# A hybrid decoder layer on one core: reordering the last K step of the input projection, and starting two branches inside it

## Chip, core and metric

The kernel runs on one core of a Trainium2 chip. The metric is the device time of one execution in microseconds (us); lower is better. Three runs of the kernel before gave 1704.4, 1707.65 and 1708.73 us, so the median is 1707.65 us.

## What is computed

One decoder layer on 256 prompt tokens and 8 sample tokens (264 columns), model width 2048, everything in float32. Cut to what matters here:

```python
mod = silu(c) @ w_mod + b_mod                      # six sections of 2048
h = rmsnorm(x, g_mix) * (1 + sc_m) + sh_m
proj = h @ w_in                                    # u_a, u_b, v_b, z, xbc, dt, three gates
o_a = s5_branch(u_a, ...)                          # scan over time, then y * sigmoid(y @ w_glu)
o_b = gelu(u_b) * (w_s @ rmsnorm(gelu(v_b)) + b_s) # gMLP
o_c = ssd_branch(z, xbc, dt, ...)                  # conv, chunked scan, gate, norm
merged = g_a*(o_a @ w_pa) + g_b*(o_b @ w_pb) + g_c*(o_c @ w_pc)
x = x + gt_m * (merged @ w_out)
x = x + gt_f * conv_ffn(rmsnorm(x) * (1 + sc_f) + sh_f)
```

## The kernel before

**Weights.** Activations lie with features on partitions and the 264 tokens along the free dimension. A weight piece is 512 KB (four k tiles of 128 by 256 columns). `load_w` (line 284) loads it through SP into one of three `raw` buffers; ACT copies it to `hi` (line 255 is the helper `act`) and DVE, or POOL for every second piece of the streams named in `SHARED` (`w_pb`, `w_ga`, `w_pa`, `w_z`), subtracts to get `lo` (line 243, helper `sub`). `gemm_piece` (305) then issues 24 matmuls of 264 columns: hi by xh, hi by xl, lo by xh (line 258, helper `mm`). `prefetch` keeps loads and splits three pieces ahead.

**K steps.** The first part of the input projection cannot wait for the whole normalised input, because the modulation that it needs is itself computed from streamed weights. So it runs in the five steps of `KSTEPS` (line 36): k tiles 0-1, 2-3, 4-7, 8-11, 12-15. Each step goes through all 16 column groups of 256 and a narrow one, `DT` (64), in the order given by `cuts` (67), and adds its part to the accumulators `acc` (0 to 2 hold xbc, 3 u_a, 4 v_b, 5 u_b, 6 and 7 the first half of the gate of branch B) on DVE (line 240, helper `add`). In a step, the modulation of the next four k tiles is loaded and multiplied (`mod_gen`, 369).

**The rest.** After the last K step come the streams `w_gb` (16 pieces here), `w_pb` (8), `w_ga` (32), `w_pa` (8), `w_z` (16), `w_gc`, `w_pc`, `w_out`, then the feed-forward part. The other four sections of the modulation run beside them (`mod_sec`, 387; its matmuls are named `mods`).

**Background work.** The branches are Python generators in the queue `fill`, run strictly one after the other. `pump` (449) is called behind each piece with a credit in us; it issues generator steps, each with its own price (`yield 2.3`), until the credit is used; `yield BRK` ends the turn. `finish` (463) issues all that is left of one. A K step of four k tiles gives 0.3 x 4 = 1.2 us per group (1198), the streams behind it 2.2 us per piece (`PACE`, 1246). The generators touched here:

- `gen_s5_prep` (556): constants of S5, small DVE operations, loads of 128, 512 and 512 KB through SP, eight PE transposes. Queued in the step with k0 = 8 (1176).
- `gen_s5_tables` (640): four tables of cosines and sines, built by 168 POOL operations. Queued in the last step (1178), completed behind it (1206).
- `gen_gm` (775): the gMLP branch. Two loads (512 and 256 KB), a POOL select, gelu on ACT, the norm, four transposes `vT` and 16 matmuls `gms` per half.
- `gen_s5` (666): 16 state tiles. Per tile PE reads in (4 matmuls `pg<-acc,bbT`), DVE rotates (`ta<-pg`, `tb<-pg`), scans (line 733) and rotates back together with POOL (`s5hh`), PE reads out (`s5py`). A tile is priced 1.3 + 2.3 + 0.6 us and has a `BRK`. Behind the last tile: gelu, the split into `s5h` and `s5l`, and two pieces of `w_glu`, loaded when they are reached (765), not ahead.
- `gen_ssd` (830): convolution of xbc, the softplus and cumulative sum of dt, then two chunks.

`gen_gm`, `gen_s5` and `gen_ssd` are queued in this order behind the last K step (1242 to 1244); `finish(g_gm)` stands ahead of `w_pb`, `finish(g_s5)` ahead of `w_pa`, `finish(g_ssd)` behind `w_z`. All engine orders come out of a scheduler at build time that works through this program order by priority, with buffers and estimated durations; each engine then runs its list in order.

Of the kernel before, what the change touches and what calls it, by code (L numbers as in the profile page):

```python
# [36 lines left out]

# ---------------------------------------------------------------- host layout

# [12 lines left out]
def _feat(a):  # L52
    """(F,) -> [128, F/128], feature on partitions."""
    return np.asarray(a).reshape(-1, P).T


def _pieces(w, kk):
    """[K, N] -> [N/256 * K/(128 kk), 128, kk*256], column groups outermost."""
    K, N = w.shape
    a = w.reshape(K // (P * kk), kk, P, N // 256, 256).transpose(3, 0, 2, 1, 4)  # L60
    return np.ascontiguousarray(a).reshape(-1, P, kk * 256)
# [4 lines left out]

def cuts(nk):
    """Column groups of one step (DT: the narrow one), in pieces of at most four k tiles x groups."""
    n = 4 // nk
    out = [[DT]]  # L70
    for lo, hi in ((0, 6), (6, 12 + NGA)):
        out += [list(range(a, min(a + n, hi))) for a in range(lo, hi, n)]
    return out[1:] + out[:1]


def pack(i):
# [22 lines left out]
    for s, (k0, nk) in enumerate(KSTEPS):  # L99
        r = slice(P * k0, P * (k0 + nk))  # L100
        v = [np.concatenate([dtp[r] if g == DT else wa[r, 256 * g:256 * g + 256] for g in gs], 1)
             for gs in cuts(nk)]
        A[f"w_a{s}"] = np.concatenate([a.reshape(nk, P, -1).transpose(1, 0, 2).reshape(-1) for a in v])
# [89 lines left out]

# ---------------------------------------------------------------- the kernel

def build(tc, I, O):
# [57 lines left out]
    def act(o, a, f, **kw):  # L254
        S.activation(o, a, f, **kw)  # L255
# [3 lines left out]

    # ---- constants  # L260
    ident = cst.tile([P, P], F32, name="ident")
# [20 lines left out]

    # ---- helpers
    def load_w(src, kk, n, e=V):
# [15 lines left out]
    def take():  # L300
        """Next piece of the main stream; loads and splits run ahead of its use."""
        prefetch()
        return ahead.popleft()

    def gemm_piece(ps, w, X, k0, kk, nt, start, stop, c0=0):
        """ps[:, j, :T] += W[k0.., tile j]^T X, W and X each in two f32r parts."""
        hi, lo = w
        for j in range(nt):
            c = slice(c0 + 128 * j, c0 + 128 * j + 128)
            for i in range(kk):  # L310
                xh, xl = X(k0 + i)
                o = ps[:, j, :T]
                mm(o, hi[:, i, c], xh, start and i == 0, False)
                mm(o, hi[:, i, c], xl, False, False)
                mm(o, lo[:, i, c], xh, False, stop and i == kk - 1)

    def rstd_of(ps, n, width=T):
        """1/sqrt(ps/n + eps), one Newton step after the table."""
        v = W("rv", [P, width])
        ts(v, ps, 1.0 / n, ALU.mult, EPS, ALU.add)  # L320
        y = W("ry", [P, width])
        act(y, v, AF.Sqrt)
        V.reciprocal(y, y)
        t = W("rt", [P, width])
        stt(t, y, -0.5, y, ALU.mult, ALU.mult)
        mult(t, t, v)
        r = W("rstd", [P, width])
        stt(r, t, 1.5, y, ALU.add, ALU.mult)
        return r
# [4 lines left out]

    # ---- modulation
    mod_ps, mod_ev = {}, {}

    def mod_load(s_, nk, sec, i):
        """8 / nk k tiles of 128 nk columns"""
        raw = RM("rawm")  # L340
        nc.sync.dma_start(raw, I[f"w_m{s_}"][2 * nk * sec + i])
        return raw.rearrange("p (k n) -> p k n", k=8 // nk)
# [26 lines left out]
    def mod_gen(s_, k0, nk, depth):  # L369
        """sc, then sh, of nk feature tiles, at least four k tiles per step; the loads run ahead of their use."""  # L370
        pp = max(2, nk // 2)
        steps = [(sec, i) for sec in (1, 0) for i in range(0, 2 * nk, pp)]
        got = deque()
        for j in range(len(steps) + depth):
            if j < len(steps):
                sec, i = steps[j]
                got.append([mod_load(s_, nk, sec, i + p_) for p_ in range(pp)])
            if j >= depth:
                sec, i = steps[j - depth]
                for p_, raw in enumerate(got.popleft()):  # L380
                    mod_part(sec, i + p_, nk, raw)
                if i + pp == 2 * nk:
                    with tc.high_priority():
                        mod_fin(sec, k0, 128 * nk)
            yield pp / max(1, nk // 2)

    def mod_sec(sec, depth=1, get=RM, kk=2):
        """One section of 2048 columns, kk k tiles per step; its four 512-column chunks sit in four column groups."""
        ps = None
# [33 lines left out]
    def modulate(k0, nk, xq, rstd, gname, s_sh, s_sc, hi, lo):  # L423
        """hi + lo = x * rstd * (g (1 + sc)) + sh for feature tiles k0.. k0+nk-1 (of one slot)"""
        sh = mod[:, 16 * s_sh + k0:16 * s_sh + k0 + nk, :]
# [18 lines left out]

    # ---- background work, paced against the weight pieces
    fill = deque()
# [42 lines left out]

    # ---- first RMS norm  # L490
    rstd0 = cst.tile([P, T], F32, name="rstd0")

    def sum_tok(pt, sqs, first, last):
        """sums of squares, tokens on partitions; the three columns share a bank, so only the first starts"""
        for i, sq in enumerate(sqs):
            for b, t0 in enumerate((0, 128, T - 128)):
                mm(pt[:, b:b + 1], sq[:, t0:t0 + 128], ones[:, :1], first and i == 0 and b == 0,
                   last and i == len(sqs) - 1)
        return pt

    def rstd_tok(pt, PM=PM):
        """1/sqrt(mean + eps) of every token, on all partitions, by way of tokens on partitions"""
        w = W("rtk", [P, 4, 3])
# [25 lines left out]

    # ---- S5: parameters  # L530
    def exp_acc(o, a, n):
# [130 lines left out]

    # ---- branch A: S5
    oA = {}
# [108 lines left out]

    # ---- branch B: gMLP
    def gen_gm(ub, vb):
# [50 lines left out]

    # ---- branch C: SSD
    xsb = {}

    def gen_ssd(raws, dtr):  # L830
# [29 lines left out]

        # dt = softplus(raw + bias), da = -exp(a_log) dt
        dt = cst.tile([16, T], F32, name="dt")
# [47 lines left out]
        yield BRK  # L910
        # token-major B, CB^T
        Bt = W("Bt", [P, 2, 2, 128])
# [175 lines left out]

    # ---- segment A: modulated norm and the first column tiles, one quarter of K at a time
    XH, XL, acc = [], [], []  # L1090
# [3 lines left out]
    for s_, (k0, nk) in enumerate(KSTEPS):  # L1094
        o = 0
        for i, gs in enumerate(cuts(nk)):
            n = 128 if gs == [DT] else 256 * len(gs)
            e = G if (i % 2 == 1 if nk == 1 else i % 3 == 1 and nk == 2) else V
            queue.append((I[f"w_a{s_}"][o:o + P * nk * n].rearrange("(p n) -> p n", p=P), nk, n, e))
            o += P * nk * n  # L1100
# [3 lines left out]
    def lead_order(n):  # L1104
        """the first groups side by side, one piece of K after the other"""
        m = KD // 4
        return [g * m + q for q in range(m) for g in range(LEAD)] + list(range(LEAD * m, n))
# [30 lines left out]
    def warm(n, src=None):  # L1138
        """matmuls that keep the tensor engine's clock up while the first loads arrive"""
        for _ in range(n):  # L1140
# [27 lines left out]
    for s_, (k0, nk) in enumerate(KSTEPS):  # L1168
        nxt = None
        if s_ + 1 < NS:  # L1170
            nxt = step_mods(s_ + 1)
            mods.append(nxt)
            if s_ == 0:
                prefetch()
                mpump(DEPTH(1))
        if k0 == 8:
            fill.append(g_prep)
        if s_ == NS - 1:
            fill.append(g_tab)
        for g, first, o in [(g, i == 0, 256 * i) for gs in cuts(nk) for i, g in enumerate(gs)]:  # L1180
            ps = PG()
# [14 lines left out]
            if s_ == NS - 1 and g >= 12:  # L1196
                act(dst, dst, AF.Sigmoid)
            pump(0.3 * nk)
            mpump(0.8 if KSTEPS[min(s_ + 1, NS - 1)][1] > 1 else 0.8 / 2)
# [3 lines left out]
        if nxt:  # L1203
            mfinish(nxt)
            step_h(s_ + 1)
    finish(g_tab)

    # ---- the rest of the input projection, with the branches behind it
    MS = (1, RM, 2) if 2 == 2 else (2, RM, 1)
# [31 lines left out]

    g_s5, g_gm = gen_s5(acc[3]), gen_gm(acc[5], acc[4])
    g_ssd = gen_ssd(acc[:3], acc_dt)
    fill.extend([g_gm, g_s5, g_ssd])

# [48 lines left out]

    # ---- output projection, residual
    x1 = [Q("x1") for _ in range(4)]
    for j in range(4):
        nc.sync.dma_start(x1[j], I["x"][j])
    def residual(g, src, xt, s_gt, ssq, scale=None):
        """xt += gate * src for two feature tiles; sums of squares, then the scaling of the final norm"""  # L1300
        c0 = 2 * (g % 2)
# [49 lines left out]

    # ---- ConvFFN
    AH, AL = {}, {}
# [78 lines left out]
```

## Time and profile before

| | |
|---|---|
| median of three runs | 1707.65 us (1704.4 to 1708.73) |
| span of the profiled execution, first to last instruction | 1703.2 us |
| its own time with what lies around the span | not given apart from the runs, whose lowest is 1704.4 us |
| busy PE, DVE, ACT, POOL | 1655.1, 1125.4, 735.0, 285.6 us |
| weight loads on PE (PEld) | 1523.5 us |
| last K step, `w_gb`, S5 tiles, `w_pa` in this trace | about 230 to 279, 279 to 341, 315 to 468, 523 to 557 us |

The span is read as one line of time from 0 to 1703.2 us. An engine's busy time says how long it had an instruction in work; a matmul's row runs from its start to its modelled end, and matmuls overlap, so the distance of starts is the pace. "idle before <-" tells what ended an engine's idle time.

### The profile page before, as it was taken

What the parts mean: (1) busy time and instruction counts of PE and PEld (TensorE: products, weight loads), DVE (VectorE), ACT (ScalarE), POOL (GpSimd) and SP (SyncE); (2) the same over time, 40 slices, a digit from 0 to 9 for tenths busy, and PEclk for the clock granted to TensorE, in tenths of its full rate; (3) what the DMA queues carried; (4) which work ended last, traced back from release to release, by engine and by line L of the source; (5) the groups of instructions that cost most, each with busy time, mean ns of one, the idle gap of its engine ahead of it and who ended that gap; (6) DMA issues with size and microseconds to landing.
All of it is one profiled execution on the core that took longest, in us unless ns stands there. A gap on an engine that the chain in (4) does not pass through costs nothing.

```text
span 1703.2 us, 32237 instructions
## 1 busy us (share of the span) xinstructions
PE 1655.1 (97%) x13172; PEld 1523.5 (89%) x13172; DVE 1125.4 (66%) x1897; ACT 735.0 (43%) x962; POOL 285.6 (17%) x323
## 2 busy tenths in 40 slices
PE   7999999999999999999999999999999999999996
PEld 5778899877777799999988999999999999999996
DVE  3455877899969648875547766666544566666553
ACT  4423346322255533354335544545433455455442
POOL 0200079266734324200000000000000000000000
PEclk8999999999999999999999999999999999999998
DMA  8867985666467857868995666545555555555552
GB/s 319 303 230 289 342 286 168 223 244 226 165 215 269 303 210 259 287 213 299 332 348 195 241 217 225 177 174 194 178 185 180 179 186 181 182 185 182 181 185 89
DMA packets 107267, 385.12 MB, mean 226 GB/s; under 512 B 12192, under 2 KB 13408, under 8 KB 107120
## 3 DMA queue, kind: packets, MB, share of 16 engines
q1 hardware_dynamic: 103968, 372.58, 61.7%
q0 software_dynamic: 3152, 10.50, 1.7%
q8 instruction: 103, 1.69, 0.4%
q14 instruction: 44, 0.36, 0.1%
HBM read 374.56 MB, written 8.46 MB: 225 GB/s over the span
## 4 chain that ended last, share of the span: by engine, by line
PE 77%; DVE 13%; DMA 4%; issue 3%; ACT 2%; POOL 1%; SPq 0%; DVEq 0%; ACTq 0%; POOLq 0%
PE pg L258 70%; DVE lo L243 3%; PE mods L258 3%; PE mod L258 2%; DVE gg L733 2%; DVE ta L240 1%; ACT hi L255 1%; DMA raw<-in_w_z 1%; DMA raw<-in_w_up 1%; DVE ta L237 1%; DVE cv L246 1%; POOL hup L237 1%; DMA csb<-csd 1%; DVE hst L246 0%; DVE tb L237 0%
## 5 line engine op out<-in xcount | busy, mean ns | idle before, releaser
L243 DVE TENSOR_TENSOR lo<-raw,hi 128x1024 fp32r<-128x1024 f32 x457 | 578.7, 1267 | 398.6 <-ACT hi L255 387.7
L255 ACT ACTIVATE hi<-raw 128x1024 fp32r<-128x1024 f32 (+1 forms) x495 | 520.7, 1054 | 726.9 <-PE pg L258 509.2
L258 PE MATMUL pg<-hh,hi 128*128 128x264 f32 x1408 | 399.5, 284 | 0.5 <-DVE fcv L246 0.5
L258 PE MATMUL pg<-hh,lo 128*128 128x264 f32 x1408 | 398.5, 283 | 0.0
L258 PE MATMUL pg<-hl,hi 128*128 128x264 f32 x1408 | 398.5, 283 | 0.0
L258 PE MATMUL pg<-xh,hi 128*128 128x264 f32 x1296 | 376.4, 291 | 2.8 <-ACT xh L255 1.7
L258 PE MATMUL pg<-xh,lo 128*128 128x264 f32 x1296 | 370.3, 286 | 4.8 <-DVE lo L243 4.8
L258 PE MATMUL pg<-xl,hi 128*128 128x264 f32 x1296 | 369.1, 285 | 0.1
L258 PEld LDWEIGHTS pg<-xh,hi 128*128 128x128 f32 x1296 | 245.0, 189 | 39.7 <-issue 22.3
L258 PEld LDWEIGHTS pg<-hh,hi 128*128 128x128 f32 x1408 | 264.5, 188 | 10.8 <-issue 9.2
L258 PEld LDWEIGHTS pg<-hl,hi 128*128 128x128 f32 x1408 | 264.4, 188 | 0.8 <-DVE hl L246 0.8
L258 PEld LDWEIGHTS pg<-hh,lo 128*128 128x128 f32 x1408 | 264.6, 188 | 0.0
L258 PEld LDWEIGHTS pg<-xh,lo 128*128 128x128 f32 x1296 | 244.9, 189 | 9.5 <-DVE lo L243 6.5
L258 PEld LDWEIGHTS pg<-xl,hi 128*128 128x128 f32 x1296 | 245.2, 189 | 5.7 <-issue 4.9
L258 PE MATMUL pg<-fl,hi 128*128 128x264 f32 x704 | 200.0, 284 | 0.0
L258 PE MATMUL pg<-fh,hi 128*128 128x264 f32 x704 | 199.8, 284 | 0.0
L258 PE MATMUL pg<-fh,lo 128*128 128x264 f32 x704 | 199.4, 283 | 0.0
L258 PEld LDWEIGHTS pg<-fh,hi 128*128 128x128 f32 x704 | 132.5, 188 | 0.0
L258 PEld LDWEIGHTS pg<-fl,hi 128*128 128x128 f32 x704 | 132.4, 188 | 0.0
L258 PEld LDWEIGHTS pg<-fh,lo 128*128 128x128 f32 x704 | 132.3, 188 | 0.0
L243 POOL TENSOR_TENSOR lo<-raw,hi 128x1024 fp32r<-128x1024 f32 x38 | 100.0, 2635 | 160.1 <-ACT hi L255 136.1
L1381 POOL DMA_DIRECT2D out_utail<-ut x4 | 2.2, 542 | 597.9 <-ACT ut L255 597.9
(328 smaller groups left out, 2119.0 us busy)
## 6 DMA issues: line engine op xcount, KB each, us to landing
raw<-in_w_up SPq DMA_DIRECT2D x176, 512.0 KB, 3.5
raws<-in_w_mod SPq DMA_DIRECT2D x128, 512.0 KB, 5.9
raw<-in_w_down SPq DMA_DIRECT2D x88, 512.0 KB, 3.5
raw<-in_w_a SPq DMA_DIRECT2D x64, 512.0 KB, 5.2
rawm<-in_w_m SPq DMA_DIRECT2D x64, 512.0 KB, 7.2
raw<-in_w_ga SPq DMA_DIRECT2D x32, 512.0 KB, 3.5
raw<-in_w_gc SPq DMA_DIRECT2D x32, 512.0 KB, 4.1
raw<-in_w_out SPq DMA_DIRECT2D x32, 512.0 KB, 4.5
```

Source lines behind the costliest of these rows:

```text
L237: e.tensor_tensor(o, a, b, op=ALU.mult)
L240: e.tensor_tensor(o, a, b, op=ALU.add)
L243: e.tensor_tensor(o, a, b, op=ALU.subtract)
L246: V.scalar_tensor_tensor(o, a, s, b, op0=op0, op1=op1)
L255: S.activation(o, a, f, **kw)
L258: TE.matmul(o, l, r, start=start, stop=stop, skip_group_check=True, **kw)
L733: V.tensor_tensor_scan(gg[:, i, k], rb, ta[:, i, k], ini[:, i:i + 1] if c else 0.0, op0=ALU.mult, op1=ALU.add)
L1381: nc.gpsimd.dma_start(O["utail"][s], ut)
```

## The change

The last K step takes its columns in the order v_b, u_b, u_a, xbc, DT, gates, one group per piece as before. When the group that completes u_a (g = 7) is done, gMLP and S5 are queued, with eleven of the 17 groups still to come. S5's constants are queued one K step earlier (k0 = 4), its tables one step earlier (k0 = 8), and both are completed ahead of the last step's first group. SSD is queued behind the step as before. The host packs the weights in the new order; comments and docstrings are dropped.

```diff
-def cuts(nk):
-    n = 4 // nk
+def cuts(s):
+    if s == len(KSTEPS) - 1:
+        return [[g] for g in (8, 9, 10, 11, 6, 7, 0, 1, 2, 3, 4, 5, DT, *range(12, 12 + NGA))]
+    n = 4 // KSTEPS[s][1]
...
+        if k0 == 4:
+            fill.append(g_prep)
         if k0 == 8:
-            fill.append(g_prep)
+            fill.append(g_tab)
         if s_ == NS - 1:
-            fill.append(g_tab)
+            finish(g_prep)
+            finish(g_tab)
...
             if s_ == NS - 1 and g >= 12:
                 act(dst, dst, AF.Sigmoid)
+            if s_ == NS - 1 and g == 7:
+                g_s5, g_gm = gen_s5(acc[3]), gen_gm(acc[5], acc[4])
+                fill.extend([g_gm, g_s5])
             pump(0.3 * nk)
...
-    finish(g_tab)
...
-    g_s5, g_gm = gen_s5(acc[3]), gen_gm(acc[5], acc[4])
     g_ssd = gen_ssd(acc[:3], acc_dt)
-    fill.extend([g_gm, g_s5, g_ssd])
+    fill.append(g_ssd)
```

## Rows read from the trace of the kernel before

**Rows 1.** Page, busy us, share of the span and instructions of each engine.
```profile
PE 1655.1 (97%) x13172; PEld 1523.5 (89%) x13172; DVE 1125.4 (66%) x1897; ACT 735.0 (43%) x962; POOL 285.6 (17%) x323
```

**Rows 2.** Busy time by stretch: length, engines with counts, granted clock, DMA share, GB/s.
```profile
350.00:375.00 25.00, 25.00 (x184) 19.40 (x183) 24.86 (x42) 5.99 (x9) 16.34 (x14) 1.00 0.55 191
475.00:480.00 5.00, 3.11 (x7) 1.34 (x7) 2.65 (x3) 4.68 (x5) 0.00 (x0) 0.59 0.60 217
480.00:485.00 5.00, 5.00 (x32) 4.29 (x34) 0.96 (x1) 0.73 (x1) 0.00 (x0) 0.72 0.33 105
525.00:550.00 25.00, 22.04 (x180) 18.45 (x179) 24.62 (x35) 11.89 (x13) 12.67 (x7) 1.00 0.75 286
```

**Rows 3.** Instruction groups, PE, 343 to 450 us: count, busy us, mean ns, idle before.
```profile
L258 PE MATMUL pg<-xh,hi 128*128 128x264 f32 x128 | 37.0, 289 | 0.8 <-DVE gate L237 0.8
L258 PE MATMUL pg<-acc,bbT 32*128 32x264 f32 x48 | 13.8, 407 | 0.0
```

**Rows 4.** Instructions in order of time, PE: read-ins of S5 tiles 0, 2, 15.
```profile
315.15 1.15 PE L258 MATMUL pg<-acc,bbT 32*128 32x264 f32 x4
...
331.20 1.15 PE L258 MATMUL pg<-acc,bbT 32*128 32x264 f32 x4
...
447.98 1.15 PE L258 MATMUL pg<-acc,bbT 32*128 32x264 f32 x4
```

**Rows 5.** Instructions in order of time, DVE: first rotations of tiles 0, 1, 2, 15; splits.
```profile
316.34 0.69 DVE L237 TENSOR_TENSOR ta<-pg,tab 128x512 f32<-128x512 f32 x1 [0.96 <-PE pg L258]
...
325.29 0.69 DVE L237 TENSOR_TENSOR ta<-pg,tab 128x512 f32<-128x512 f32 x1 [0.77 <-PE pg L258]
...
329.43 1.23 DVE L243 TENSOR_TENSOR lo<-raw,hi 128x1024 fp32r<-128x1024 f32 x1
...
332.46 0.69 DVE L237 TENSOR_TENSOR ta<-pg,tab 128x512 f32<-128x512 f32 x1
...
453.79 2.32 DVE L243 TENSOR_TENSOR lo<-raw,hi 128x1024 fp32r<-128x1024 f32 x1
456.03 0.68 DVE L237 TENSOR_TENSOR ta<-pg,tab 128x512 f32<-128x512 f32 x1
```

**Rows 6.** Waits of PE, 450 to 500 us: us in total, times, longest.
```profile
PE pg L258 <- ACT s5h L255: 3.1, 1, 3.1
PE s5py L258 <- POOL s5hh L243: 2.5, 2, 1.9
PE s5py L258 <- POOL s5hh L240: 1.0, 1, 1.0
```

**Rows 7.** Instructions in order of time, ACT, 474 us: what stands ahead of `s5h`.
```profile
474.81 1.06 ACT L255 ACTIVATE hi<-raw 128x1024 fp32r<-128x1024 f32 x1 [2.32 <-DMA raw<-in_w_glu]
```

**Rows 8.** Instructions in order of time, ACT and PE: gelu of v_b, and gMLP's first transpose.
```profile
260.80 1.09 ACT L255 ACTIVATE acc<-acc 128x1056 f32<-128x1056 f32 x1
...
296.42 0.33 PE L806 MATMUL vT<-ident,acc 128*128 128x128 f32 x1 [1.50 <-DVE acc L246]
```

**Rows 9.** Instructions in order of time, PE and DVE, inside `w_pa`.
```profile
528.50 0.39 PE L258 MATMUL pg<-oah,lo 128*128 128x264 f32 x1 [1.42 <-POOL lo L243]
...
534.82 0.39 PE L258 MATMUL pg<-oah,hi 128*128 128x264 f32 x1 [1.54 <-ACT gate L255]
...
533.47 2.88 DVE L892 TENSOR_TENSOR_SCAN csum<-ones,da 16x128 f32<-16x128 f32 x2
...
536.33 0.68 DVE L237 TENSOR_TENSOR gate<-gate,pg 128x528 f32<-128x528 f32 x1
```

**Rows 10.** Waits of DVE, 560 to 610 us: us in total, times, longest.
```profile
DVE de L243 <- DMA csb<-csd: 5.9, 2, 5.6
```

**Rows 11.** Busy time by stretch, columns as in rows 2: third K step, last, gMLP.
```profile
108.00:158.00 50.00, 49.26 (x371) 39.21 (x371) 28.36 (x38) 17.01 (x20) 0.00 (x0) 1.00 0.85 318
230.60:284.00 53.40, 53.40 (x440) 53.27 (x439) 36.51 (x37) 27.22 (x29) 53.40 (x123) 1.00 0.68 234
284.00:316.30 32.30, 30.80 (x261) 27.81 (x263) 21.99 (x31) 14.80 (x17) 12.92 (x24) 1.00 0.54 195
```

More of the change, by code (lines that the diff above doesn't have):

```diff
@@ L101, in pack @@
         v = [np.concatenate([dtp[r] if g == DT else wa[r, 256 * g:256 * g + 256] for g in gs], 1)
-             for gs in cuts(nk)]
+             for gs in cuts(s)]
         A[f"w_a{s}"] = np.concatenate([a.reshape(nk, P, -1).transpose(1, 0, 2).reshape(-1) for a in v])
@@ L1095, in build @@
         o = 0
-        for i, gs in enumerate(cuts(nk)):
+        for i, gs in enumerate(cuts(s_)):
             n = 128 if gs == [DT] else 256 * len(gs)
@@ L1175, in build @@
                 mpump(DEPTH(1))
+        if k0 == 4:
+            fill.append(g_prep)
         if k0 == 8:
-            fill.append(g_prep)
+            fill.append(g_tab)
         if s_ == NS - 1:
-            fill.append(g_tab)
-        for g, first, o in [(g, i == 0, 256 * i) for gs in cuts(nk) for i, g in enumerate(gs)]:
+            finish(g_prep)
+            finish(g_tab)
+        for g, first, o in [(g, i == 0, 256 * i) for gs in cuts(s_) for i, g in enumerate(gs)]:
             ps = PG()
```

## Prediction

> **What bounds the kernel now.** I read the page's busy times first: PE is at work for 97% of the span [rows 1], so a change can win only what PE loses in waits, plus a fall of its clock. Then I went through the stretches that the change touches and asked in each who is late.
>
> Beside the S5 tiles both engines look full: in 25 us PE is busy for 25.00 and DVE for 24.86 [rows 2]. The groups of PE decide: in the 107 us from 343 to 450 its idle time before weight matmuls is 0.8 us and before the read-ins nothing [rows 3]. PE sets the pace there. But DVE is a little too slow to follow, and the reader can see it fall behind. A read-in of four matmuls takes 1.08 us; it ends at 316.23 for tile 0, at 332.28 for tile 2, at 449.06 for tile 15 [rows 4]. DVE takes these results up at 316.34, 332.46 and 456.03 [rows 5]. The lag is 0.1, then 0.2, then 7.0 us. It starts to grow when POOL begins to split the pieces of `w_pb`: a DVE split that took 1.23 us now takes 2.32 [rows 5], and from tile 2 to tile 15 the lag gains 6.8 us in 13 tiles, 0.52 each. PE pays when it needs S5's results: it waits 2.5 and 1.0 us for the last rotations and 3.1 us for `s5h`, 6.6 in all [rows 6], about the lag. Behind that the granted clock is 0.59 and 0.72 over two stretches of 5 us [rows 2], part of them at the 1.2 GHz level, which costs (0.41 + 0.28) x 5 = 3.4 us.
>
> gMLP costs PE one wait of 1.50 us, where the transposes stand in its list before DVE has scaled v_b [rows 8]. In `w_pa` PE waits 1.42 us for a split and 1.54 us for a PSUM bank [rows 9], while DVE is busy for 24.62 of 25 us [rows 2]: a scan of SSD's dt stands ahead of the epilogue that frees the bank [rows 9].
>
> **The change, part by part.** First the order of issue, from the prices in the code. Before, gMLP uses pieces 0 to 9 of `w_gb`, a state tile uses two pieces (4.2 us of price against 2 x 2.2), so tiles 0 to 2 lie in `w_gb` and 13 lie in `w_pb` and `w_ga`, where POOL splits every second piece. After, gMLP is issued in the eleven groups left in the K step and the first piece of `w_gb`; tiles start with piece 2. Everything of S5 and SSD moves eight pieces forward: seven tiles lie in `w_gb`, nine behind it. No matmul is added or removed.
>
> *gMLP in the K step.* Its DVE work is at most the 22.0 us that DVE is busy from 284 to 316 us, less eight splits of 1.23, about 12 us; in the last K step DVE is idle for 53.4 - 36.5 = 16.9 us [rows 11], and the tables' POOL work leaves that step. So it hides, closely: with PSUM in three buffers, DVE may be two groups late before PE stops. With 1.2 us of credit per group the transposes come four groups behind the norm instead of two pieces, so the 1.50 us wait should go. Bounds: a gain of 1.5, or a loss of 1.5 if the wait returns in the K step; I take **-1.5**, because the distance doubles.
>
> *Seven tiles without POOL splits instead of three.* The lag at tile 15 becomes 0.2 + 9 x 0.52 = 4.9 us instead of 7.0, and PE's waits behind S5 shrink with it. Bounds: nothing, if the waits are latency and not lag, and 6.6 us, if all of them go. I take **-2.1**. The chain that ends in the 3.1 us wait stays: ACT's copy into `s5h` stands behind a split that waited 2.32 us for a piece of `w_glu` [rows 7], loaded only then. So I leave the clock's fall in: 0, with 3.4 us as the other end.
>
> *SSD eight pieces earlier.* Convolution and dt then meet `w_ga`, whose epilogue is on ACT, not `w_pa`, whose epilogue needs DVE (0.68 us for the multiplication [rows 9] and an addition of the same size, every piece). That takes away the two waits, 2.96 us. In return the first chunk meets `w_pa`. Bounds: a gain of 3.0, and a loss of 5.6, the wait of DVE for SSD's broadcast loads [rows 10] with an epilogue behind it. I take **-2.0**, near the first end: PE had no wait beside the convolution in `w_ga`.
>
> *S5's constants and tables a step earlier.* Nothing. The constants' small operations meet a DVE that is busy for 28.4 of 50 us; their loads of 1.15 MB go through SP past the pieces and modulation of the third K step and need 3.6 us at the 318 GB/s seen there, with 15% of the DMA time free and three pieces loaded ahead [rows 11]. The cost is 0 to 3.6 us and I take 0. The tables need at most 53.4 + 12.9 = 66 us of POOL [rows 11]; in the fourth K step POOL has no splits, and S5 reads the first table some 40 us later. gMLP's select and its two loads (768 KB) go with it, on queues that have room.
>
> The sum is -1.5 - 2.1 - 2.0 = -5.6 us: a span of 1697.6 instead of 1703.2. The median of the runs lies 4.45 us above this span, so I say **1702.0 us**.
>
> **Rivals.** *S5's tail closes.* If 2 us less lag is enough for the `w_glu` load to come before PE needs it, all 6.6 us of waits and the 3.4 us of the clock go: -1.5 - 6.6 - 3.4 - 2.0 = -13.5, 1694.2 us. For it: the waits add up to the lag. Against it: the 2.32 us wait for `w_glu` [rows 7] does not depend on lag.
>
> *DVE, not PE, bounds the tiles.* On DVE a tile takes 332.46 - 325.29 = 7.17 us in `w_gb`, and (456.03 - 332.46) / 13 = 9.51 beside POOL's splits [rows 5]. If PE followed, four tiles moved would give 4 x 2.34 = 9.4 us instead of 2.1: 1694.8 us. Against it stands PE's idle time of 0.8 us [rows 3]. The Trainium skill (Perfetto Trace Analysis, section Identifying the Most-Contended Engine) speaks for this rival: there matmul busy time is a bad measure of room and LDWEIGHTS busy share a good one. The 19.40 of 25 us here would by that rule be room of 22%; but a read-in loads only 32 rows and its matmuls start every 0.27 us, so I read little room in it.
>
> *Only gMLP's wait goes.* The tail and SSD's waits keep their size at their new place: 1706.2 us.
>
> *Slower: SSD's first chunk in `w_pa`.* DVE waits 5.6 us for a broadcast load [rows 10]; in `w_z` nothing of PE's hung on it, since that epilogue is on ACT. In `w_pa` the epilogues that free PSUM stand behind it. If both chunks' loads are late there, 2 x 5.6 = 11.2 us come and SSD's 2.0 don't: -3.6 + 11.2 = +7.6, 1715.3 us. It decides once DVE reaches the chunk more than two pieces before the load has landed.
>
> *The change does not do what it says.* The scheduler already put gelu of v_b into the last K step, at 260.80 us [rows 8], though the program has it behind; if it orders PE by its own estimate, the new place changes little: 1707.7 us.
>
> **How the numbers follow.** Forecast 0.38, tail closes 0.18, DVE bounds 0.07, only gMLP 0.17, slower 0.15, no effect 0.05. A measurement of this kernel can tell about 0.3%, 5.1 us, from no change, so faster begins at 1702.5. The forecast's own range, 1698 to 1705, straddles that: I give 0.23 of its 0.38 to faster. Faster: 0.23 + 0.18 + 0.07 = 0.48; same: 0.15 + 0.17 + 0.05 = 0.37; slower 0.15. The range 1694 to 1712 takes in all cases but the slower one.
>
> **What would show it.** Right: `vT` without a wait and before 284 us; seven read-ins before `w_pb`'s first matmul; a lag of about 5 us at tile 15; fewer than 6.6 us of waits behind it; no waits inside `w_pa`. Wrong: a lag that grows in `w_gb` too, PE waits for accumulator additions in the last K step, waits for `s5h` as long as before, or DVE idle for `csb` inside `w_pa`.

## The result and the profile after

The change made the kernel slower. Twelve executions of the changed kernel have a median of 1710.53 us (1707.26 to 1715.5), twelve of the kernel before on the same chip 1700.38 us (1697.37 to 1708.73): a ratio of 1.0058, 95% interval 1.0047 to 1.007, about 10 us. The three executions shown ahead of the prediction (median 1707.65) were on the high side; a comparison within one chip counts. The two profiled executions have spans of 1703.2 and 1709.7 us, so the traces show 6.5 of those 10 us. The rest is spread: a run's time is 1.7 us more than its span (1711.42 and 1709.7 us in the kernel after), so the profiled execution of the kernel before took, as an estimate, 1704.9 us, 4.5 above its median, that of the kernel after 0.9 above its own.

On the page of the kernel after, the first section answers to [rows 1]:

```profile
PE 1659.7 (97%) x13172; PEld 1529.9 (89%) x13172; DVE 1124.4 (66%) x1897; ACT 735.3 (43%) x963; POOL 274.6 (16%) x323
```

The matmuls are the same 13172, and the share of PE is the same 97%. The page doesn't say where the time went; a table by stage does. The edges of the stages are found by counting the matmuls on the normalised input (`pg<-xh,hi`), 132 in a K step of four k tiles. The rows are: third K step, fourth K step, from the last K step to the first matmul of `w_pc`, and the rest. Columns as in [rows 2]. Kernel before:

```profile
108.10:169.90 61.80, 61.12 (x468) 51.07 (x469) 39.09 (x62) 21.68 (x28) 0.00 (x0) 1.00 0.82 305
169.90:229.30 59.40, 59.40 (x479) 51.50 (x478) 50.77 (x142) 23.65 (x30) 4.73 (x24) 1.00 0.88 321
229.30:735.30 506.00, 485.63 (x3745) 429.40 (x3743) 407.83 (x646) 208.03 (x244) 256.64 (x278) 0.99 0.66 236
735.30:1703.20 967.90, 953.22 (x7790) 921.27 (x7790) 582.45 (x968) 438.92 (x600) 7.90 (x10) 0.99 0.59 205
```

Kernel after:

```profile
107.50:173.80 66.30, 65.60 (x476) 52.59 (x477) 53.67 (x152) 24.07 (x33) 2.11 (x11) 1.00 0.81 292
173.80:240.90 67.10, 61.70 (x470) 53.40 (x469) 42.92 (x51) 19.62 (x24) 61.17 (x159) 0.95 0.71 264
240.90:741.90 501.00, 481.63 (x3746) 431.14 (x3744) 398.63 (x648) 210.13 (x246) 187.89 (x132) 0.99 0.68 240
741.90:1709.70 967.80, 953.76 (x7790) 921.80 (x7790) 582.80 (x968) 438.69 (x600) 7.89 (x10) 0.99 0.61 205
```

The stretch for which I had forecast a gain of 5.6 us became 5.0 us shorter. The loss is ahead of it: 66.3 instead of 61.8 us in the third K step, 67.1 instead of 59.4 in the fourth, 12.2 together. These are the two steps into which S5's constants and tables were moved, and there I had written "Nothing".

**Third K step.** PE isn't waiting there: it is busy for 65.60 of 66.30 us, so it does the same work more slowly. The groups of PE in this stage name the work, the matmuls of the modulation. First the kernel before, then the kernel after (count, busy us, mean ns):

```profile
L258 PE MATMUL mod<-rawm,cs 128*32 128x512 f32 x64 | 10.6, 605 | 0.0
```

```profile
L261 PE MATMUL mod<-rawm,cs 128*32 128x512 f32 x64 | 13.7, 605 | 0.0
...
L635 PE MATMUL bbt<-ident,bb 128*128 128x128 f32 x8 | 1.2, 272 | 0.0
```

The same 64 records of 605 ns cover 3.1 us more. In order of time it is seen why. Kernel before, one batch:

```profile
127.40 1.06 PE L258 MATMUL mod<-rawm,cs 128*32 128x512 f32 x8
```

Kernel after, the same place:

```profile
126.79 1.05 PE L261 MATMUL mod<-rawm,cs 128*32 128x512 f32 x4
...
128.21 1.05 PE L261 MATMUL mod<-rawm,cs 128*32 128x512 f32 x4
```

Eight of these narrow matmuls next to each other take 1.06 us, and four take 1.05. A batch of eight that is cut in two by other matmuls costs about 1 us more. Besides one batch that both kernels cut into two and six, the kernel before cuts one batch in this step, the kernel after four: 3.1 us. The eight transposes of the constants, 1.2 us, come on top, moved here from the fourth step: 4.3 of the 4.5 us.

**Fourth K step.** Here it is waits and clock. Instructions of DVE in order of time, kernel after:

```profile
211.57 7.60 DVE L246 TENSOR_TENSOR lo<-raw,hi 128x1024 fp32r<-128x1024 f32 x1
219.09 0.69 DVE L243 TENSOR_TENSOR acc<-acc,pg 128x528 f32<-128x528 f32 x1
219.71 1.22 DVE L246 TENSOR_TENSOR lo<-raw,hi 128x1024 fp32r<-128x1024 f32 x1
...
233.96 1.28 DVE L249 SCALAR_TENSOR_TENSOR ht<-x,gs,rstd 128x256 f32<-128x256 f32 x1 [6.49 <-POOL tab L243]
```

One split takes 7.60 us, its neighbour 1.22. And 15 us later DVE waits 6.49 us for the last of POOL's tables, with an instruction that uses nothing of the tables: it got the buffer of their scratch `tt`, which comes out of the pool of small buffers. Instructions of POOL around the long split:

```profile
211.55 0.32 POOL L246 TENSOR_TENSOR tab<-tab,tt 128x64 f32<-128x64 f32 x1
...
217.35 0.74 POOL L243 TENSOR_TENSOR tab<-tab,tt 128x256 f32<-128x256 f32 x1
218.05 1.34 POOL L240 TENSOR_TENSOR tt<-tab,trig 128x4 f32<-128x4 f32 x2
```

POOL issues one table operation behind the other, without a gap, and the split ends within the first of them that is itself late: two operations of 128x4 in 1.34 us. The held splits of runs 2 and 4, below, end within such a pair too (1.33 us each). What hangs on the split, from the waits of all engines between 209 and 238 us (us in total, times, longest):

```profile
ACT hi L258 <- DVE lo L246: 6.8, 1, 6.8
DVE ht L249 <- POOL tab L243: 6.5, 1, 6.5
...
PE modT L365 <- ACT mev L258: 3.7, 1, 3.7
...
PE pg L261 <- DVE acc L243: 1.7, 1, 1.7
```

ACT has no free buffer for its next piece until the split is done, the copy of the modulation stands behind it, and PE waits 3.7 us for that copy. It then waits 1.7 us for DVE. Within the first wait the clock falls to its 1.2 GHz level:

```profile
222.80:229.60 6.80, 5.21 (x24) 5.21 (x25) 3.62 (x10) 3.17 (x7) 6.80 (x22) 0.50 0.93 343
```

PE is busy for 5.21 of these 6.8 us (the rest is waiting, counted already), and at half clock half of that, 2.6 us, is lost. The three together are 8.0 us; less the 1.2 us of transposes that left the step, that is 6.8 of the 7.7 us. What the other 0.9 us are is not shown.

**Behind it.** What was to show the forecast right did, for the most part. PE in order of time, kernel after, to be read against [rows 8] and [rows 4]:

```profile
277.44 0.60 PE L809 MATMUL vT<-ident,acc 128*128 128x128 f32 x4
...
359.63 1.15 PE L261 MATMUL pg<-acc,bbT 32*128 32x264 f32 x4
361.72 0.39 PE L261 MATMUL pg<-obh,hi 128*128 128x264 f32 x1
...
432.10 1.15 PE L261 MATMUL pg<-acc,bbT 32*128 32x264 f32 x4
```

The transposes wait for nothing and begin before 284 us; the eighth read-in stands ahead of `w_pb`'s first matmul (I had said seven); tile 15 is read in by 432.10 + 1.08 = 433.18. DVE takes it up at

```profile
437.76 0.68 DVE L240 TENSOR_TENSOR ta<-pg,tab 128x512 f32<-128x512 f32 x1
```

a lag of 4.6 us, forecast 4.9, before 7.0 [rows 5] (1.08 us is the pace of a read-in, as in the prediction). PE's waits from 450 to 500 us, against [rows 6]:

```profile
PE pg L261 <- ACT s5h L258: 3.1, 1, 3.1
PE pg L261 <- ACT hi L258: 1.8, 1, 1.8
```

4.9 instead of 6.6 us, a gain of 1.7 where I had 2.1. But from 500 to 600 us there are new waits of PE:

```profile
PE ypy L261 <- DVE L L240: 2.7, 1, 2.7
PE tk L907 <- DVE dt L249: 2.4, 1, 2.4
PE tk L907 <- DVE csum L895: 1.6, 1, 1.6
PE hst L261 <- DVE yv L249: 1.1, 2, 0.6
```

They are SSD's own instructions on PE, `tk` ahead of `w_pa`, the others in it and right behind it, 7.8 us in all. In the kernel before, the two waits of [rows 9] and four of 1.0 us or less stood here.

### The profile page after: what moved, and what is told of

Read it like the earlier page. It is cut to its first block, busy times and chain, and to the rows that moved or that the text cites. A ratio compares the mean times of both kernels' runs of the same rounds, so it can differ in the third digit from the quotient of the medians.

```text
span 1709.7 us, 32238 instructions
## 1 busy us (share of the span) xinstructions
PE 1659.7 (97%) x13172; PEld 1529.9 (89%) x13172; DVE 1124.4 (66%) x1897; ACT 735.3 (43%) x963; POOL 274.6 (16%) x323
## 4 chain that ended last, share of the span: by engine, by line
PE 61%; DVE 6%; DMA 2%; issue 1%; ACT 1%; POOL 0%; DVEq 0%; SPq 0%; ACTq 0%; POOLq 0%
PE pg L261 57%; PE mods L261 2%; DVE lo L246 1%; DVE cv L249 1%; DVE hst L249 1%; DMA raw<-in_w_up 1%; DMA raw<-in_w_gc 1%; DMA csb<-csd 0%; DMA out_ssm_s<-hst 0%; ACT hi L258 0%; DVE dp L249 0%; DVE yd L1059 0%; DVE hup L240 0%; PE sst L261 0%; POOL hup L240 0%
## 5 line engine op out<-in xcount | busy, mean ns | idle before, releaser
L258 ACT ACTIVATE hi<-raw 128x1024 fp32r<-128x1024 f32 (+2 forms) x495 | 520.1, 1053 | 746.7 <-PE pg L261 505.0
L261 PE MATMUL pg<-xl,hi 128*128 128x264 f32 x1296 | 373.0, 288 | 0.1
L246 POOL TENSOR_TENSOR lo<-raw,hi 128x1024 fp32r<-128x1024 f32 x38 | 94.7, 2494 | 168.1 <-ACT hi L258 138.3
```

The costliest lines, as they stand in the source:

```text
L246: e.tensor_tensor(o, a, b, op=ALU.subtract)
L261: TE.matmul(o, l, r, start=start, stop=stop, skip_group_check=True, **kw)
```

## The experiments

All kernels were compared with the kernel before on the same chip. The scratch, constants and tables are those of S5. "After" is the changed kernel.

**1. The early branches alone.** After, with constants and tables queued where they were (the constants are still completed ahead of the last step's first group, the tables when the branches are queued):

```diff
-        if k0 == 4:
-            fill.append(g_prep)
         if k0 == 8:
-            fill.append(g_tab)
+            fill.append(g_prep)
         if s_ == NS - 1:
             finish(g_prep)
-            finish(g_tab)
+            fill.append(g_tab)
...
             if s_ == NS - 1 and g == 7:
+                finish(g_tab)
```

> The changed kernel with S5's constants back in the step with k0 = 8 and the tables back in the last K step; the new column order and the early start of gMLP and S5 stay. My theory (the loss lies in the third and fourth K steps, +4.5 and +7.7 us in the trace, and comes from the constants and tables; the early branches themselves win about 5 us): ratio to before 0.997, about 5 us faster, and the last K step begins near 229 us, as before. Rival (SSD's first chunk in the w_pa stream costs the time): still slower than before, ratio 1.004 or more, with the loss inside w_pa.

Measured: 1717.19 us, ratio 1.0096 (1.0081 to 1.0112). The theory missed. Both K steps had their old length, but the last step did not. Waits from 262 to 290 us:

```profile
DVE gmd L255 <- POOL tab L243: 20.1, 1, 20.1
PEld pg L261 <- DVE acc L243: 16.2, 1, 16.2
PE pg L261 <- DVE acc L243: 16.0, 1, 16.0
```

and the clock behind it:

```profile
272.10:289.20 17.10, 4.10 (x18) 4.10 (x19) 5.21 (x11) 0.00 (x0) 12.60 (x42) 0.50 0.10 29
```

The scratch buffer again: now gMLP's first DVE instruction (`gmd`) gets it, with all additions and splits queued behind. So this run says nothing yet of what the early start is worth, and the next step was to give the scratch a place of its own.

**2. The step up alone.** The kernel before, with constants and tables queued one step earlier and completed ahead of the last step, branches as before:

```diff
-        if k0 == 8:
+        if k0 == 4:
             fill.append(g_prep)
-        if s_ == NS - 1:
+        if k0 == 8:
             fill.append(g_tab)
+        if s_ == NS - 1:
+            finish(g_prep)
+            finish(g_tab)
```

> The kernel before with one part of the change alone: S5's constants in the step with k0 = 4, the tables in the step with k0 = 8, both completed ahead of the last K step; column order and start of the branches as before. My theory: about 12 us slower than before, ratio 1.007, less some 2 us because gMLP's norm no longer runs beside the tables; the last K step begins near 241 us. Rival (the step up costs nothing, as I predicted): ratio 1.000, last K step begins near 229 us.

Measured: 1714.38 us, ratio 1.0071 (1.0052 to 1.009), as the theory had it: this part alone costs as much as the whole change or more (the intervals overlap). The modulation matmuls of the third step are again 13.7 us, and in the fourth one split is again held:

```profile
179.57 8.30 DVE L243 TENSOR_TENSOR lo<-raw,hi 128x1024 fp32r<-128x1024 f32 x1 [2.89 <-ACT hi L255]
```

**3. The tables alone back.** After, with the tables where they were, constants still one step up:

```diff
-        if k0 == 8:
-            fill.append(g_tab)
         if s_ == NS - 1:
             finish(g_prep)
-            finish(g_tab)
+            fill.append(g_tab)
...
             if s_ == NS - 1 and g == 7:
+                finish(g_tab)
```

> The changed kernel with the tables alone back in the last K step; S5's constants stay in the step with k0 = 4. My theory (two separate costs): only the third K step's 4.5 us stay, so ratio 1.000 to before, 7 to 8 us faster than the changed kernel; the fourth K step takes about 59 us instead of 67. Rival (the constants alone make both losses): ratio 1.005, as the changed kernel.

Measured: 1722.27 us, ratio 1.0132 (1.0111 to 1.0152). The same wait of `gmd`, 20.2 us, hides what was asked. Against run 1, which differs by the constants alone, it is 5.1 us slower: the price of the constants in the third step.

**4. Scratch of its own.** After, with

```diff
-        tt = W("tt", [P, 512])...
+        tt = cst.tile([P, 512], F32, name="tt")...
```

> The changed kernel with the tables' scratch tile in a buffer of its own instead of the shared pool of eight small buffers. My theory: in the changed kernel DVE's last scaling for the last K step waited 6.5 us for the end of POOL's tables because it got the buffer of this scratch tile; with its own buffer that wait goes, and with it some 3 to 5 us of the fourth K step's 7.7 (PE idle and the 1.2 GHz stretch behind it): ratio 1.003 to before. Rival (the wait is the shared SBUF path between POOL and DVE, not the buffer): the wait of DVE on the tables stays and the ratio is that of the changed kernel, 1.006.

Measured: 1709.64 us, ratio 1.0052 (1.0035 to 1.007). DVE's wait of 6.49 us for the tables is gone and the time is not: in the kernel after, this wait cost no more than the measurement's width. A split is held for 8.26 us as before.

**5. Early branches alone, own scratch.** Run 1 with the scratch of run 4.

> The changed kernel with S5's constants and tables back at their old places (constants in the fourth K step, tables in the last) and with the tables' scratch buffer taken from a pool of its own, so that gMLP's first VectorE instruction no longer gets that buffer. Theory (the early start itself wins about 5 us; the 16 to 20 us stall of the two runs with the tables in the last step was the shared scratch buffer alone): no VectorE wait on GpSimd at gMLP's first instruction, no TensorE gap of over 4 us between 230 and 300 us, time 0.997 of the kernel before (0.995 to 1.000), faster than either kernel. Rival (the tables and the early branches get into each other's way on VectorE and GpSimd whatever the buffer): the first scaled tile of gMLP or a split beside the tables still waits many us, a TensorE gap of over 8 us stays, time 1.005 or more.

Measured: 1711.11 us, ratio 1.0056 (1.004 to 1.0072). The wait of `gmd` went, and nearly 7 us with it, but the theory missed again; a stall of the rival's kind was there, of 5.4 us on PE instead of over 8, and with another cause than the rival had. Waits from 284 to 300 us:

```profile
DVE obl L246 <- DMA out_vn<-acc: 12.1, 1, 12.1
...
PE pg L261 <- DVE lo L246: 5.4, 1, 5.4
```

gMLP's result `obl` takes the buffer of v_b, and the last reader of v_b is an output that POOL issues, in its queue behind the tables. A second tie to the end of the tables, by way of a queue.

**6. Tables on DVE.** Run 4, with `e = V` instead of `e = G` in `gen_s5_tables`.

> The changed kernel with the scratch buffer of its own (1.005 of the kernel before as it stands) and its table operations on VectorE instead of GpSimd. Theory (a VectorE split is held up for some 8 us by GpSimd's unbroken train of table operations, which costs TensorE 4.6 us and then some clock): no split of over 2 us between 150 and 245 us, no TensorE gap of over 2 us there, the fourth K step near 61 us instead of 65.4, time 1.002 (1.000 to 1.004). Rival (the 168 small operations make VectorE late for the accumulator adds): TensorE waits for accumulator banks in the fourth step, no shorter than 65 us, time 1.005 or more.

Measured: 1702.91 us, ratio 1.0013 (1.0 to 1.0026). As the theory had it: by the ratios 6.6 us better than run 4. Third and fourth K step:

```profile
107.90:174.20 66.30, 65.61 (x476) 52.59 (x477) 54.22 (x161) 23.74 (x33) 0.00 (x0) 1.00 0.80 293
174.20:235.80 61.60, 59.19 (x471) 51.07 (x470) 56.68 (x210) 20.15 (x24) 1.97 (x1) 1.00 0.87 311
```

The fourth step is 61.6 us instead of 65.4, at full clock, and no split there takes more than 1.23 us. DVE has 56.68 us of work in 61.60, which is close to its limit, and still loses less than beside POOL's operations.

**7. The loads on another queue.** Run 4, with the three loads of the constants (`h0s5`, `bbd`, `cbd`) issued by POOL:

```diff
-        nc.sync.dma_start(h0s5, I["s5_h0"])
+        nc.gpsimd.dma_start(h0s5, I["s5_h0"])
```

> The changed kernel with the scratch buffer of its own (1.005 of the kernel before as it stands) and the three loads of S5's constants issued by GpSimd's queue instead of SyncE's. Theory (the loads on SyncE's queue shift the order of the third K step, so that modulation matmuls come in pairs, 4 to 5 us): the third step takes 62 us (61 to 63.5) instead of 66, time 1.0025 (1.001 to 1.004). Rival (it is the constants' own VectorE work and transposes that shift the order, not the loads): the third step stays at 65 us or more, time 1.004 or more.

Measured: 1698.91 us, ratio 0.9988 (0.9974 to 1.0002). The whole loss of the change is gone. Groups of PE in the third step, which takes 61.6 us:

```profile
L261 PE MATMUL mod<-rawm,cs 128*32 128x512 f32 x64 | 9.6, 605 | 0.0
```

9.6 us: apart from the one in two and six no batch is cut now, although the constants' DVE work and transposes are in this step as before. So it was the loads' place in SP's queue, not their bytes: taking it away changes the order in which the scheduler puts the modulation's matmuls. The gain of 11 us is larger than the 5 us of the step and than the theory's range. The profiled execution, at 1707.97 us the longest of twelve, can't show where the rest comes from: its fourth step still has a long split (instructions of DVE in order of time, two splits in one row) and takes 63.9 us.

```profile
177.52 7.01 DVE L246 TENSOR_TENSOR lo<-raw,hi 128x1024 fp32r<-128x1024 f32 x2
```

**8. The kernel before with the scratch of run 4.**

> The kernel before with the tables' scratch buffer in a pool of its own, nothing else. Theory (there the instruction that gets the buffer is issued only after the tables have ended, so the buffer costs it nothing): 1.000 (0.998 to 1.002). Rival (the wait for the buffer costs the kernel before a few us too, and part of any gain of the early start with the own buffer is the buffer's): 0.998 or less.

Measured: 1700.73 us, ratio 1.0003 (0.9992 to 1.0013). The buffer by itself is worth nothing; of the kernels here it costs clearly only where a branch begins before the tables end (runs 1 and 3).

**9. Loads on POOL's queue and tables on DVE.** Runs 6 and 7 together.

> The changed kernel with all three mends: scratch buffer of its own, the three loads of S5's constants on GpSimd's queue (0.9988 with these two), and the table operations on VectorE. Theory (the order of SyncE's queue costs the third K step and GpSimd's train costs the fourth, each by itself): third step 61.6 us and fourth 61.6 us, no TensorE gap of over 1.5 us before the tables' end, time 0.9975 of the kernel before (0.996 to 0.999), faster than every kernel here. Rival (the two costs overlap: with the third step short, the fourth loses to VectorE what the train cost it): fourth step 63 us or more, time 0.999 or more.

Measured: 1699.11 us, ratio 0.9986 (0.9973 to 1.0). In the trace both steps are at their old length, 61.6 and 59.5 us. In time it adds nothing that can be told from run 7. The two prices are not a plain sum: by the ratios, moving the loads gains 10.9 us with the tables on POOL (run 4 to 7) and 4.6 with them on DVE (6 to 9), and moving the tables gains 6.6 us first (4 to 6) and then 0.3 (7 to 9). Why the tables on POOL cost nothing in the median of run 7, whose trace still has a held split, is not shown.

**10. Early branches alone, both ties cut.** Run 5, with the output of v_b issued by ACT's queue:

```diff
-        nc.gpsimd.dma_start(O["vn"]...
+        nc.scalar.dma_start(O["vn"]...
```

> The changed kernel with constants and tables at their old places, the scratch buffer of its own (1.0056), and gMLP's output of vn issued by ScalarE's queue, so that it doesn't stand behind the tables on GpSimd's. Theory (the stall of 5.5 us there was VectorE waiting for a buffer whose last reader, that output, stood behind the tables; next in line is S5's first tile, which waits for the tables themselves): the 12 us wait of gMLP's split goes, VectorE waits 4 to 9 us at S5's first product instead, the TensorE gap at 284 to 300 us falls from 5.5 to 0 to 3 us, time 1.002 (1.000 to 1.004). Rival (the wait simply moves on to S5's first tile, whole): TensorE gap of 5 us or more, time 1.005 or more.

Measured: 1700.6 us, ratio 1.0001 (0.9987 to 1.0014), 9.4 us better than run 5. The wait of `obl` is gone and PE waits for nothing from 284 to 300 us; the wait for the tables that I expected next did not come. But the early start without any of the moves ahead of it gains nothing in time, though gMLP and S5 run as in the kernel after. Something behind them takes the gain back.

**11 and 12. SSD where it was.** Runs 9 and 10, with SSD put off by eight pieces:

```diff
     def gen_ssd(raws, dtr):
+        for _ in range(8):
+            yield BRK
```

> The changed kernel with all three mends (0.9986 of the kernel before) and the SSD put off by eight weight pieces, to where the kernel before has it. Theory (the SSD's earlier start gains nothing: its waits only move from the stage of w_pa to the end of w_ga and to w_z, and TensorE's clock falls to half behind them, 13.6 us at half clock between 500 and 570 us): from the start of w_ga to the start of w_gc no stretch, or one, at half clock, and time 0.996 (0.994 to 0.998). Rival (the SSD's earlier start gains the 2 us that I gave it, and the half clock comes from elsewhere): the stretches at half clock stay, the SSD's waits stand in w_pa again, time 0.9995 (0.9985 to 1.001).

> The run with constants and tables at their old places, own scratch and vn's output on ScalarE's queue (1.0001 of the kernel before), with the SSD put off by eight weight pieces. Theory as in the run beside it (the SSD's early start gains nothing and costs clock; here 10.2 us at half clock between 500 and 563 us): those stretches go, all but one at most, and time 0.9975 (0.996 to 0.999). Rival (the early SSD gains its 2 us): time 1.001 or more.

Measured: 1695.83 us, ratio 0.997 (0.9958 to 0.9983), and 1695.18 us, ratio 0.9966 (0.9954 to 0.9977). Both are faster than the kernel before, and, by the ratios, 2.7 and 6.0 us better than runs 9 and 10 (the first is about the width of the measurement, the second is clear of it). The same 85 us of the trace, first of run 9, then of run 11:

```profile
490.00:530.00 40.00, 36.28 (x284) 32.48 (x283) 27.58 (x44) 23.89 (x28) 15.06 (x9) 0.91 0.85 313
530.00:575.00 45.00, 41.83 (x319) 33.75 (x316) 37.67 (x71) 16.29 (x18) 13.08 (x7) 0.92 0.68 225
```

```profile
490.00:530.00 40.00, 38.00 (x306) 32.44 (x305) 29.01 (x48) 26.92 (x29) 15.29 (x8) 1.00 0.87 327
530.00:575.00 45.00, 45.00 (x359) 38.26 (x359) 31.59 (x56) 20.85 (x24) 17.98 (x9) 1.00 0.84 303
```

With SSD early, PE is idle for 6.89 us and its clock is 0.91 and 0.92; with SSD at its old place it is idle for 2.00 us at full clock. Run 9 has two stretches of 6.8 us at the 1.2 GHz level here, one behind the waits of `tk` and one at `ypy`:

```profile
500.70:507.50 6.80, 5.63 (x25) 5.49 (x26) 4.30 (x6) 2.21 (x4) 2.92 (x2) 0.50 0.75 251
...
558.80:565.60 6.80, 6.27 (x40) 5.40 (x41) 5.29 (x7) 1.83 (x2) 2.96 (x1) 0.50 0.20 57
```

This was the theory; the rival, that the early SSD gains 2 us, is out.

## Why the prediction was wrong

I forecast 1702.0 us, 5.6 less than the time given, with a chance of 0.15 for slower; it is slower by 10 us against the kernel before on the same chip. That 1710.53 us lies inside my range of 1694 to 1712 is luck: the range was counted from 1707.65 us, and the ratio puts the changed kernel at 1717.6 on that base.

**The step that failed: "S5's constants and tables a step earlier. Nothing."** I priced the constants by their bytes (0 to 3.6 us) and the tables by POOL's free time (nothing). Both were the wrong currency: the two steps became 12.2 us longer. The constants' loads cost by their place in SP's queue: three batches of modulation matmuls more were cut in two, and 1.2 us of transposes moved along, 4.5 us in the third step (run 7 takes it away with the loads). The tables did fit on POOL, in 62 us, but held one DVE split for 7.60 us, and PE paid 3.7 us and then clock (run 6 takes it away, 6.6 us by the ratios; with the loads moved first there is nothing left to take away in time, run 9). I had read that POOL's splits nearly double a DVE split [rows 5] and used it for the S5 tiles, and didn't ask what 168 POOL operations would do to the splits of the fourth step. Run 2 shows that this one step was enough to turn the sign: 1.0071 by itself.

The Trainium skill (SBUF — State Buffer, section Who interferes with whom) says that a DVE instruction with two SBUF inputs contends with a GpSimd instruction that reads SBUF. Of the ports that the two engines share it says that they are an exclusive lock, and, in its lines on DVE's 2-port modes, that the one that issues first has them for its whole instruction while the other is blocked. A split has two such inputs. The trace agrees that the two engines contend, but the wait is of another size: the split was held for 6.4 us more than usual, over a train of table operations of which the longest single one took 0.74 us, so by this rule, as an estimate, a lock of one instruction would have held it about a ninth as long. That it is this lock is argued from the times; run 6 shows that without the table operations on POOL no split is held. Why a train in the fourth step holds one split so long, and the trains in the last step of runs 1, 5, 10 and 12 none beyond 1.9 us, is not shown by these runs.

**gMLP in the K step, -1.5: right.** `vT` waits for nothing. In the last K step no wait of PE comes from gMLP's work.

**Seven tiles in `w_gb`, -2.1: right in mechanism, 1.7 in size.** Eight tiles lie there, the lag is 4.6 us, the waits behind S5 4.9 instead of 6.6. That the size is so near is in part luck: both waits for the last rotations, 3.5 us [rows 6], are gone, and one of 1.8 us, for ACT's copy of a piece of `w_glu`, is new. My 3.4 us for the clock's fall there, left out of the sum, were too many: PE was busy for 5.67 of the 6.83 us at that level, from 475.73 to 482.56 us, so 2.8 were lost. The rival in which the tail closes didn't come: the 3.1 us for `s5h` stand unchanged. Nor did the one in which DVE bounds the tiles.

**SSD eight pieces earlier, -2.0: wrong in sign.** I was right that the waits inside `w_pa` [rows 9] go: one of 0.5 us is left. I took the removal of two waits for a gain, without asking what is late next. The softplus and the cumulative sum of dt are the same DVE work, and `tk` needs both. Before, DVE had finished the sum at 533.47 + 2.88 = 536.35 us [rows 9], and PE came to `tk` behind it:

```profile
537.92 0.29 PE L904 MATMUL tk<-ident,dt 16*128 16x16 f32 x2
```

After, DVE is busy for 18.59 of the 19 us from 496 to 515 us (convolution, splits, dt), and PE comes to `tk` first (2.4 and then 1.6 us), as it later does to `ypy` (2.7). DVE, PE, and the stretch behind `tk` (columns as in [rows 2]), kernel after:

```profile
513.12 0.42 DVE L249 SCALAR_TENSOR_TENSOR dt<-dp,dx 16x264 f32<-16x264 f32 x1
513.59 0.29 PE L907 MATMUL tk<-ident,dt 16*128 16x16 f32 x2 [2.36 <-DVE dt L249]
516.35:519.76 3.41, 3.41 (x18) 3.41 (x17) 2.65 (x1) 0.83 (x2) 2.55 (x2) 0.50 1.02 405
```

My slower rival had put SSD's price at the broadcast loads, in `w_pa`; it was neither that place nor that mechanism. Runs 11 and 12 measure it on the mended kernels: putting SSD back gains 2.7 and 6.0 us.

**The sum.** From the last K step to `w_pc` the trace gave -5.0 against my -5.6, an agreement that is partly luck: runs 9 and 11 have -1.4 and -8.0 there (504.6 and 498.0 us against 506.0), so gMLP's and S5's early start was worth more than I said, and SSD took back what I had put down as its gain. In run 12, where the two branches begin early with both ties cut and SSD, constants and tables stay where they were, the whole is worth 5.8 us (1700.95 to 1695.18). Of the 4.45 us that I added to the span, 1.7 lie around a span; the rest was the spread of three runs, and the difference that I forecast doesn't rest on it.

## What to carry to other kernels

Work that is moved to where its engines are idle still has three prices that busy times don't show: its place in each in-order queue, the buffer pools that it shares with work of other stages (a scratch buffer tied one branch to the end of a table for 20 us), and the engine that it shares a path with. Ask of each of them before writing "nothing". And when a later stage moves up because an earlier one does, it is a change of its own: price it apart, and try it apart.

## What the runs showed of the hardware that I had not expected

Four fp32 modulation matmuls of 32 columns side by side cost PE 1.05 us and eight 1.06, so what counts is how often such a batch is interrupted. A DVE split of 1.2 us can last 7.60, 8.30 or 8.26 us while POOL issues short operations without a gap (kernel after, runs 2 and 4). The clock after a wait of PE is not the same each time: in the kernel after, half clock came for 6.8 us with the wait of 3.7 us, for 3.4 us behind the two at `tk` (2.4 and 1.6), and not at all behind the 2.7 us at `ypy`; in run 9 the wait at `ypy` (2.6) came with 6.8 us at half clock, in which PE was busy for 6.27, a loss of 3.1. So a small wait of PE may cost its length, or as much again.
